# Weight sums of the seven-product stages: from subtracts on VectorE to accumulating DMAs

## The chip, the cores and the metric

The kernel runs on one core of a Trainium2 chip. The metric is the device time of one execution in microseconds (us). A core has TensorE (PE, matmul), VectorE (DVE), ScalarE (ACT), GpSimd (POOL) and SyncE (SP), each with an instruction queue of its own that runs in order, and 16 DMA engines that all queues share.

## The reference

512 tokens of width 1024 run through a first block (three mixers, a gate, the projection `w_o`, a convolved feed-forward network with `w_down`) and through a second block of depth 2 (three branches, the projection `w_out_2`, an MLP of width 4096 with `w_mlp_out_2`). What matters here are the products that end a part and add to the residual:

```python
x = x + merged @ w_o[i]
x = x + conv_ffn(rmsnorm(x, ln2_g[i]), ...)      # (silu(a) * v) @ w_down
```

and their like in the second block. All data are 32-bit floats.

## The kernel before

Every 32-bit operand is split into a high and a low half; a product is then three matmuls (high by high, high by low, low by high). For a weight tile `raw` of 128x1024, `halve` makes both halves by `split`: ACT casts the high half (`whi`, L294), DVE subtracts it from the raw tile and leaves the low half (`wlo`, L295). There are 7 buffers for raw tiles and 5 for each kind of half, given out in turn. Tiles named `pg` hold 128x512 of tokens, features or their halves; `ax`, `mm` and `po` are banks in which PE accumulates.

The method `quick` (from L928) computes a product of 512 tokens by a weight block of `kt` x 128 rows and 1024 columns as seven products of half-size blocks instead of eight. It runs 14 times, and these are the stages of this text: `w_o` once, the feed-forward output three times (ffn 1, 2 and 3, with kt of 8, 8 and 6), `w_out_2` twice (w_out, one for each layer of the second block) and `w_mlp_out_2` eight times (the mlp stages, four for each layer). With b11, b12, b21, b22 for the four quarters of the weight block, two raw tiles each, the right operands are W1 = b11, W2 = b21, W5 = b12 - b11, W6 = W5's tile combined with b22, W3 = b22, W7 = b12's tile combined with b22, W4 = b21 combined with W6's tile. Each quarter is loaded from HBM by SP (`load`, L941), b21 twice, and each combination is a DVE subtract of a 128x1024 tile (`combine`, L949). A combination overwrites a tile in place, after the tile's halves have been made. The left operands (`Forms.make`, from L84) are combined on DVE from the features when these come out of the stage before (L89 to L92) and are split in the same way.

`product` is 24 matmuls (L959 to L961) for each of two banks, one bank for 128 tokens; `add` takes a bank into the residual on DVE (L966, or L968 where a scale is applied). The products run in the order 1, 2, 5, 6, 3, 7, 4, with the last piece of 1 and of 2 after both. Products 6, 7 and 4 go on in the banks of product 1 (`a`), product 3 in those of product 5, so that a bank must have been added before the next product may write on. A scheduler sets the order of the instructions on each engine when the kernel is built. Between product 7 and product 4 the scheduler puts matmuls of the next features (L269 to L271).

Of the kernel before, what the change touches and what calls it, by code (L numbers as in the profile page):

```python
# [13 lines left out]
ALU = mybir.AluOpType  # L14
# [21 lines left out]
class Page:  # L36


    def __init__(self, arena, i, t):
        self.arena, self.i, self.t = arena, i, t  # L40
# [30 lines left out]
class Forms:  # L71

    def __init__(self, body):
        self.body, self.raws, self.blocks, self.pages, self.half = body, [], [], [], None

# [6 lines left out]
    def make(self, r1, r2):  # L85
        B = self.body
        v, c, d = B.nc.vector, slice(0, 256), slice(256, 512)
        s, w = B.pgs(2, True)
        v.tensor_tensor(s.t[:, c], r1.t[:, d], r2.t[:, d], op=ALU.add)  # L89
        v.tensor_tensor(r1.t[:, d], r1.t[:, c], r1.t[:, d], op=ALU.subtract)  # L90
        v.tensor_tensor(s.t[:, d], s.t[:, c], r1.t[:, c], op=ALU.subtract)
        v.tensor_tensor(w.t[:, c], r2.t[:, c], s.t[:, d], op=ALU.subtract)  # L92
        out = []
        for x in (r1, r2, s):
            hi, lo = B.pair(1)
            B.split(hi[0].t, lo[0].t, x.t)
            out.append((hi[0], lo[0]))
            x.free()
        if self.half is None:
            hi, lo = B.pair(1)  # L100
            self.half = (hi[0], lo[0])
            h, o = self.half, c
            self.pages += self.half
        else:
            h, o, self.half = self.half, d, None
        B.split(h[0].t[:, o], h[1].t[:, o], w.t[:, c])
        w.free()
        self.pages += [x for y in out for x in y]
        at = lambda pg, sl: tuple(x.t[:, sl] for x in pg)
        self.blocks.append({1: at(out[0], c), 7: at(out[0], d), 2: at(out[1], c), 4: at(out[1], d), 5: at(out[2], c),  # L110
                            6: at(out[2], d), 3: at(h, o)})
# [6 lines left out]
class Body:  # L118
# [18 lines left out]
    def mm(self):  # L137
        return self.pp.tile([P, 512], F32, tag="mm", name=self.nm("mm"), bufs=3)
# [158 lines left out]
    def turn(self, srcs):  # L297

        pt = self.ax()
        for i, s in enumerate(srcs):  # L300
            self.nc.tensor.transpose(pt[:, i * P:(i + 1) * P], s, self.ident)  # L301
        return pt
# [625 lines left out]
    def quick(self, w, k0, kt, F, X, scale=1.0, rows=None, turn=None):  # L928

        nc, Ls = self.nc, F.blocks
        v = w[k0 * P:(k0 + kt) * P, :].rearrange("(i e p) n -> e p i n", e=2, p=P)
        n = kt // 2
        parts = [(a, min(a + 2, n)) for a in range(0, n, 2)]

        def load(e, h, j):
            a, b = parts[j]
            t = self.raw()[:, :(b - a) * 512]  # L940
            nc.sync.dma_start(t.rearrange("p (k n) -> p k n", n=512), v[e - 1][:, a:b, 512 * (h - 1):512 * h])  # L941
            return t

        def right(ts):
            return [x for t in ts for x in self.halve(t, 512)]

        def combine(out, x, y, op):
            for o, a, b in zip(out, x, y):
                nc.vector.tensor_tensor(o, a, b, op=op)  # L949

        def product(i, W, pss, more=False, a=0, b=n):

            mm = nc.tensor.matmul
            for q, ps in enumerate(pss):
                c = slice(q * P, (q + 1) * P)
                for k in range(a, b):
                    hi, lo = W[k]
                    uh, ul = Ls[k][i]
                    mm(ps, uh[:, c], hi, start=not more and k == 0, stop=False, skip_group_check=more)  # L959
                    mm(ps, uh[:, c], lo, start=False, stop=False, skip_group_check=more)  # L960
                    mm(ps, ul[:, c], hi, start=False, stop=k == n - 1, skip_group_check=more)  # L961

        def add(t, h, y):
            x = X[t][h].t
            if scale == 1.0:
                nc.vector.tensor_tensor(x, x, y, op=ALU.add)  # L966
            else:
                nc.vector.scalar_tensor_tensor(x, y, scale, x, op0=ALU.mult, op1=ALU.add)  # L968

        ss, xn = {}, {}  # L970

        def sums(t):
            if rows:
                ss[t] = self.st(2)
                self.square_sum(X[t][1].t, ss[t][:, 1:2])

        js = range(len(parts))
        two = range(2)
        bank = lambda: [self.ax() for _ in two]
        b11 = [load(1, 1, j) for j in js]  # L980
        W1 = right(b11)
        a = bank()

        product(1, W1, a, b=n - 1)
        W2 = right([load(2, 1, j) for j in js])
        e = [self.mm() for _ in two]
        product(2, W2, e, b=n - 1)
        product(1, W1, a, a=n - 1)
        product(2, W2, e, a=n - 1)
        b12 = [load(1, 2, j) for j in js]  # L990
        combine(b11, b12, b11, ALU.subtract)
        W5 = right(b11)
        d = bank()
        product(5, W5, d)
        for q in two:
            add(q, 0, a[q])
        W6, W3 = [], []
        for j in js:
            t = load(2, 2, j)
            combine([b11[j]], [t], [b11[j]], ALU.subtract)  # L1000
            W6 += right([b11[j]])
            combine([b12[j]], [t], [b12[j]], ALU.subtract)
            W3 += right([t])
        for q in two:
            add(q, 0, e[q])
        product(6, W6, a, more=True)
        for q in two:
            add(2 + q, 1, d[q])
        product(3, W3, d, more=True)
        for q in two:  # L1010
            add(q, 1, a[q])
        W7 = right(b12)
        for q in two:
            add(q, 1, d[q])
            sums(q)
            if rows:
                xn[q] = rows(q, ss[q])
        product(7, W7, a, more=True)
        b21 = [load(2, 1, j) for j in js]
        combine(b21, b21, b11, ALU.subtract)  # L1020
        W4 = right(b21)
        for q in two:
            add(2 + q, 1, a[q])
            sums(2 + q)
            if turn:
                turn(q, xn[q])
        product(4, W4, a, more=True)
        for q in two:
            add(2 + q, 0, a[q])
            if rows:  # L1030
                xn[2 + q] = rows(2 + q, ss[2 + q])
        self.free(F)
        return lambda: [turn(t, xn[t]) for t in (2, 3)] if turn else None
# [727 lines left out]
```

## Time and profile before

| | before |
|---|---|
| median of 3 runs | 2857.28 us (2855.76 to 2858.98) |
| the profiled execution | 2858.8 us, span 2857.0 us |
| PE busy | 2803.2 us (98%) |
| DVE busy | 2012.7 us (70%) |
| ACT busy | 1316.8 us (46%) |
| POOL busy | 386.9 us (14%) |
| the 112 subtracts L949 on DVE | 134.1 us |

The profile is of one execution. Its busy shares are means over the whole span; what a stage waits for is read in the timeline, where a row gives the start, the duration, the engine, the line and the operation, and in square brackets the idle time of the engine ahead of it with what ended that. PE starts the next matmul before the last has left, so that the duration of one matmul (0.39 us) is longer than the distance between two.

### The profile page before, as it was taken

The page shows a single profiled execution, that of the slowest core. Times are in us where ns is not written, and L with a number is a line of the kernel's source. Part 1 is how long each engine was busy: PE and PEld are TensorE (multiplying, and loading weights), DVE is VectorE, ACT ScalarE, POOL GpSimd, SP SyncE. Part 2 cuts the span into 40 slices and gives each one's busy share as a digit, 9 for nine tenths or more (in the row PEclk, how much of TensorE's full clock was granted, in tenths as well). Part 3 has the DMA queues.
Part 4 walks back from the last instruction along what each step waited for, and adds up shares of the span by engine and source line. Part 5 has one row for each costly group of instructions (what it writes and reads, how often), then busy time and mean ns, then how long its engine had stood idle before and what let it go on. Part 6 is the DMA issues. An engine that isn't in the chain of part 4 may idle for free.

```text
span 2857.0 us, 36632 instructions
## 1 busy us (share of the span) xinstructions
PE 2803.2 (98%) x13639; PEld 2344.4 (82%) x13639; DVE 2012.7 (70%) x3585; ACT 1316.8 (46%) x2285; POOL 386.9 (14%) x414
## 2 busy tenths in 40 slices
PE   8999999999999999999999999999999999999999
PEld 7888888888878777888888788888888878788887
DVE  4346466758788786865767887777775767877777
ACT  4344245434444355553455444445554356444444
POOL 0002102400000005210631000002321343000000
PEclk9999999999999999999999999999999999999999
DMA  7243332234232433122222523344232222334432
GB/s 224 84 125 98 105 96 66 81 103 150 87 111 82 136 109 115 60 88 82 75 60 59 155 90 96 117 129 157 72 92 62 75 75 59 106 108 125 132 119 67
DMA packets 225655, 288.19 MB, mean 101 GB/s; under 512 B 17770, under 2 KB 155332, under 8 KB 225476
## 3 DMA queue, kind: packets, MB, share of 16 engines
q1 hardware_dynamic: 212288, 272.77, 31.3%
q10 hardware_dynamic: 13187, 13.08, 1.5%
q8 instruction: 107, 1.75, 0.3%
q14 instruction: 73, 0.59, 0.1%
HBM read 276.30 MB, written 11.67 MB: 101 GB/s over the span
## 4 chain that ended last, share of the span: by engine, by line
PE 85%; DVE 8%; POOL 3%; DMA 2%; issue 1%; ACT 1%; ACTq 0%; SPq 0%; POOLq 0%; DVEq 0%
PE mm L270 16%; PE mm L269 16%; PE mm L271 16%; PE ax L959 4%; PE ax L961 4%; PE ax L960 4%; PE mm L280 4%; PE mm L282 4%; PE mm L281 4%; PE ax L301 3%; DVE wlo L295 2%; POOL stats L312 1%; PE po L1343 1%; PE ax L1247 1%; PE ax L1248 1%
## 5 line engine op out<-in xcount | busy, mean ns | idle before, releaser
L295 DVE TENSOR_TENSOR wlo<-raw,whi 128x1024 fp32r<-128x1024 f32 (+3 forms) x554 | 668.9, 1214 | 314.5 <-ACT whi L294 309.5
L294 ACT CAST whi<-raw 128x1024 fp32r<-128x1024 f32 (+3 forms) x554 | 569.4, 1032 | 652.3 <-PE mm L270 353.6
L269 PE MATMUL mm<-uh,whi 128*128 128x512 f32 (+1 forms) x1792 | 686.4, 384 | 3.9 <-ACT uh L294 3.9
L270 PE MATMUL mm<-ul,whi 128*128 128x512 f32 (+1 forms) x1792 | 684.8, 382 | 3.6 <-DVE stats L311 1.8
L271 PE MATMUL mm<-uh,wlo 128*128 128x512 f32 (+1 forms) x1792 | 683.7, 383 | 0.0
L269 PEld LDWEIGHTS mm<-uh,whi 128*128 128x128 f32 x1792 | 336.9, 188 | 69.9 <-ACT uh L294 5.3
L270 PEld LDWEIGHTS mm<-ul,whi 128*128 128x128 f32 x1792 | 337.8, 189 | 68.3 <-DVE ul L295 2.6
L271 PEld LDWEIGHTS mm<-uh,wlo 128*128 128x128 f32 x1792 | 337.9, 189 | 65.2 <-issue 1.2
L280 PE MATMUL mm<-whi,uh 128*128 128x512 f32 (+3 forms) x736 | 279.8, 382 | 1.1 <-ACT uh L294 0.8
L282 PE MATMUL mm<-whi,ul 128*128 128x512 f32 (+3 forms) x736 | 278.3, 379 | 2.4 <-DVE ul L295 2.4
L281 PE MATMUL mm<-wlo,uh 128*128 128x512 f32 (+3 forms) x736 | 278.5, 379 | 0.4 <-DVE wlo L295 0.4
L959 PE MATMUL ax<-whi,pg 128*128 128x512 f32 x660 | 253.6, 392 | 8.2 <-DVE pg L966 4.2
L960 PE MATMUL ax<-wlo,pg 128*128 128x512 f32 x660 | 255.7, 390 | 0.0
L961 PE MATMUL ax<-whi,pg 128*128 128x512 f32 x660 | 252.9, 392 | 1.0 <-DVE pg L295 1.0
L312 POOL TENSOR_TENSOR stats<-stats,mhalf 128x1 f32<-128x1 f32 (+3 forms) x84 | 91.0, 1087 | 1193.5 <-DVE stats L327 612.8
L294 ACT CAST pg<-pg 128x512 fp32r<-128x512 f32 (+2 forms) x264 | 145.4, 574 | 140.4 <-DVE pg L1660 44.8
L301 PE MATMUL ax<-c_k_ident,pg 128*128 128x128 f32 x993 | 151.6, 279 | 25.4 <-DVE pg L335 10.1
L295 DVE TENSOR_TENSOR pg<-pg,pg 128x512 fp32r<-128x512 f32 (+2 forms) x264 | 160.3, 629 | 6.2 <-ACT pg L294 5.8
L301 PEld LDWEIGHTS ax<-c_k_ident,pg 128*128 128x128 f32 x993 | 123.5, 144 | 49.1 <-POOL pg L1212 11.0
L282 PEld LDWEIGHTS mm<-whi,ul 128*128 128x128 f32 x736 | 139.3, 189 | 25.6 <-DVE ul L295 3.1
L280 PEld LDWEIGHTS mm<-whi,uh 128*128 128x128 f32 x736 | 139.7, 190 | 24.6 <-ACT uh L294 1.2
L281 PEld LDWEIGHTS mm<-wlo,uh 128*128 128x128 f32 x736 | 139.7, 190 | 23.1 <-DVE wlo L295 0.6
(264 smaller groups left out, 4147.6 us busy)
## 6 DMA issues: line engine op xcount, KB each, us to landing
raw<-in_w_in_dram SPq DMA_DIRECT2D x180, 512.0 KB
raw<-in_w_mlp_out_dram SPq DMA_DIRECT2D x80, 512.0 KB
raw<-in_w_mlp_in_dram SPq DMA_DIRECT2D x64, 512.0 KB
raw<-in_ffn_w_up_dram SPq DMA_DIRECT2D x44, 512.0 KB
raw<-in_ffn_w_down_dram SPq DMA_DIRECT2D x25, 512.0 KB
raw<-in_w_out_dram SPq DMA_DIRECT2D x20, 512.0 KB
raw<-in_w_branch_dram SPq DMA_DIRECT2D x16, 512.0 KB
raw<-in_w_o_dram SPq DMA_DIRECT2D x10, 512.0 KB
```

What stands on the lines that cost most here:

```text
L269: mm(ps, hi[:, cols], uh, start=k == 0, stop=False)
L270: mm(ps, hi[:, cols], ul, start=False, stop=False)
L271: mm(ps, lo[:, cols], uh, start=False, stop=k == nk - 1)
L280: mm(ps, uh, hi, start=k == 0, stop=False)
L281: mm(ps, uh, lo, start=False, stop=False)
L282: mm(ps, ul, hi, start=False, stop=k == n - 1)
L294: self.nc.scalar.copy(hi, src)
L295: self.nc.vector.tensor_tensor(lo, src, hi.bitcast(F32), op=ALU.subtract)
L301: self.nc.tensor.transpose(pt[:, i * P:(i + 1) * P], s, self.ident)
L959: mm(ps, uh[:, c], hi, start=not more and k == 0, stop=False, skip_group_check=more)
L960: mm(ps, uh[:, c], lo, start=False, stop=False, skip_group_check=more)
L961: mm(ps, ul[:, c], hi, start=False, stop=k == n - 1, skip_group_check=more)
```

## The change

The right operands are now sums, made by DMAs that add what they fetch to what stands in the tile. x holds b11 at first; after its halves are made (W1), a DMA from GpSimd's queue adds b12 (W5 = b11 + b12), then b22 (W6), then b21 (W4). A second pair of tiles z holds b22 (W3), and b12 is added to it (W7). W2 = b21 has tiles of its own. All 112 DVE subtracts at L949 are gone. A stage with two raw tiles per quarter now has 6 loads on SP and 8 accumulating DMAs on GpSimd (`onto`) where it had 10 loads. So that the sums serve, signs move: two subtracts of `Forms.make` become scalar_tensor_tensor with a factor of -1, another swaps its operands, and `add` subtracts in the right half of the columns. The matmuls are the same in number and shape. Lines behind L73 move by one, those of `product` and `add` by five (L964 to L966, L971 and L973); the accumulating DMA is L942.

```diff
-        v.tensor_tensor(s.t[:, c], r1.t[:, d], r2.t[:, d], op=ALU.add)
+        v.tensor_tensor(s.t[:, c], r2.t[:, d], r1.t[:, d], op=ALU.subtract)
...
-        v.tensor_tensor(s.t[:, d], s.t[:, c], r1.t[:, c], op=ALU.subtract)
-        v.tensor_tensor(w.t[:, c], r2.t[:, c], s.t[:, d], op=ALU.subtract)
+        v.scalar_tensor_tensor(s.t[:, d], s.t[:, c], -1.0, r1.t[:, c], op0=ALU.mult, op1=ALU.subtract)
+        v.scalar_tensor_tensor(w.t[:, c], r2.t[:, c], -1.0, s.t[:, d], op0=ALU.mult, op1=ALU.subtract)
...
+        def move(eng, t, e, h, j, **kw):
+            a, b = parts[j]
+            eng.dma_start(t.rearrange("p (k n) -> p k n", n=512), v[e - 1][:, a:b, 512 * (h - 1):512 * h], **kw)
+            return t
...
+        def onto(ts, e, h):
+            for j, t in enumerate(ts):
+                move(nc.gpsimd, t, e, h, j, accum_op=ALU.add)
...
-        def combine(out, x, y, op):
-            for o, a, b in zip(out, x, y):
-                nc.vector.tensor_tensor(o, a, b, op=op)
...
-                nc.vector.tensor_tensor(x, x, y, op=ALU.add)
+                nc.vector.tensor_tensor(x, x, y, op=ALU.subtract if h else ALU.add)
...
-        b11 = [load(1, 1, j) for j in js]
-        W1 = right(b11)
+        x = [load(1, 1, j) for j in js]
+        W1 = right(x)
+        onto(x, 1, 2)
...
-        b12 = [load(1, 2, j) for j in js]
-        combine(b11, b12, b11, ALU.subtract)
-        W5 = right(b11)
+        W5 = right(x)
+        onto(x, 2, 2)
...
-        for j in js:
-            t = load(2, 2, j)
-            combine([b11[j]], [t], [b11[j]], ALU.subtract)
-            W6 += right([b11[j]])
-            combine([b12[j]], [t], [b12[j]], ALU.subtract)
-            W3 += right([t])
+        z = [load(2, 2, j) for j in js]
+        W6 = right(x)
+        onto(x, 2, 1)
+        W3 = right(z)
+        onto(z, 1, 2)
...
-        W7 = right(b12)
+        W7 = right(z)
...
-        b21 = [load(2, 1, j) for j in js]
-        combine(b21, b21, b11, ALU.subtract)
-        W4 = right(b21)
+        W4 = right(x)
```

The first place is PE in ffn 1, from the last matmuls of product 1 (into `ax716` and `ax717`) to the first of product 6, which writes on in `ax716`. Before:

```order
L960 MATMUL ax733_6820<-wlo731_6816,pg508_6723 128x512
L961 MATMUL ax716_6741<-whi714_6737,pg505_6716 128x512
L961 MATMUL ax717_6742<-whi714_6737,pg505_6716 128x512
L961 MATMUL ax732_6819<-whi730_6815,pg509_6724 128x512
L961 MATMUL ax733_6820<-whi730_6815,pg509_6724 128x512
L959 MATMUL ax716_6741<-whi735_6850,pg456_6209 128x512
```

Now, where the same banks are called `ax712` and `ax713`:

```order
L966 MATMUL ax712_6735<-whi710_6729,pg505_6708 128x512
L966 MATMUL ax713_6736<-whi710_6729,pg505_6708 128x512
L964 MATMUL ax727_6810<-whi722_6799,pg474_6373 128x512
L964 MATMUL ax726_6809<-whi724_6803,pg508_6715 128x512
...
L965 MATMUL ax727_6810<-wlo725_6804,pg508_6715 128x512
L966 MATMUL ax727_6810<-whi724_6803,pg509_6716 128x512
L964 MATMUL ax712_6735<-whi730_6841,pg456_6201 128x512
```

More of product 5 (the banks `ax732` and `ax733` before, `ax726` and `ax727` now) stands between the two: 13 matmuls lie between the last one into the first bank and the first one of product 6, where 3 did.

The second place is DVE in the second mlp stage, around the adds of product 1's banks (`ax1612`, `ax1613`; now `ax1588`, `ax1589`). Before:

```order
L295 TENSOR_TENSOR wlo1634_15263<-raw1630_15254,whi1633_15262 128x1024
L966 TENSOR_TENSOR pg1095_13646<-pg1095_13646,ax1612_15148 128x512
L966 TENSOR_TENSOR pg1097_13648<-pg1097_13648,ax1613_15149 128x512
L949 TENSOR_TENSOR raw1645_15368<-raw1645_15368,raw1607_15138 128x1024
L966 TENSOR_TENSOR pg1095_13646<-pg1095_13646,mm1620_15180 128x512
L295 TENSOR_TENSOR wlo1637_15270<-raw1607_15138,whi1636_15269 128x1024
L966 TENSOR_TENSOR pg1097_13648<-pg1097_13648,mm1621_15181 128x512
L966 TENSOR_TENSOR pg1100_13651<-pg1100_13651,ax1628_15226 128x512
L295 TENSOR_TENSOR wlo1639_15275<-raw1635_15266,whi1638_15274 128x1024
L966 TENSOR_TENSOR pg1102_13653<-pg1102_13653,ax1629_15227 128x512
L295 TENSOR_TENSOR wlo1641_15333<-raw1622_15212,whi1640_15332 128x1024
L295 TENSOR_TENSOR wlo1643_15337<-raw1623_15214,whi1642_15336 128x1024
```

Now (`raw1582` and `raw1583` are x, `raw1604` and `raw1605` z):

```order
L296 TENSOR_TENSOR wlo1607_15209<-raw1582_15088,whi1606_15208 128x1024
L971 TENSOR_TENSOR pg1095_13614<-pg1095_13614,ax1588_15102 128x512
L296 TENSOR_TENSOR wlo1609_15213<-raw1583_15090,whi1608_15212 128x1024
L971 TENSOR_TENSOR pg1097_13616<-pg1097_13616,ax1589_15103 128x512
L971 TENSOR_TENSOR pg1095_13614<-pg1095_13614,mm1596_15134 128x512
L296 TENSOR_TENSOR wlo1611_15219<-raw1604_15204,whi1610_15218 128x1024
L971 TENSOR_TENSOR pg1100_13619<-pg1100_13619,ax1602_15176 128x512
L971 TENSOR_TENSOR pg1097_13616<-pg1097_13616,mm1597_15135 128x512
L296 TENSOR_TENSOR wlo1613_15223<-raw1605_15206,whi1612_15222 128x1024
...
L296 TENSOR_TENSOR wlo1615_15283<-raw1604_15204,whi1614_15282 128x1024
...
L296 TENSOR_TENSOR wlo1617_15287<-raw1605_15206,whi1616_15286 128x1024
```

W6's two low halves stand at the first two adds, then W3's two, then W7's; W3's first low half has about the place that the L949 had.

The third place is POOL's queue in the first layer of the second block, between the powers of the norm (`mhalf`) ahead of the four mlp stages and what follows. Before, nothing of those stages stands there:

```order
L1575 TENSOR_SCALAR pg1036_13017<-pg1036_13017,stats_116 128x512
L312 TENSOR_TENSOR stats_116<-stats_116,mhalf_144 128x1 x8
L312 TENSOR_TENSOR stats_116<-stats_116,mhalf_144 128x8
L1196 TENSOR_TENSOR pg1348_16833<-pg1348_16833,hg1809_16776 128x512
L1211 TENSOR_TENSOR pg1348_16833<-pg1350_16842 128x8x8
```

Now:

```order
L313 TENSOR_TENSOR stats_116<-stats_116,mhalf_144 128x1 x4
L942 DMA raw1510_14460<-in_w_mlp_out_2_dram 128x2x512
L942 DMA raw1511_14462<-in_w_mlp_out_2_dram 128x2x512
L942 DMA raw1510_14460<-in_w_mlp_out_2_dram 128x2x512
L942 DMA raw1511_14462<-in_w_mlp_out_2_dram 128x2x512
L942 DMA raw1510_14460<-in_w_mlp_out_2_dram 128x2x512
L942 DMA raw1511_14462<-in_w_mlp_out_2_dram 128x2x512
L942 DMA raw1532_14576<-in_w_mlp_out_2_dram 128x2x512
L942 DMA raw1533_14578<-in_w_mlp_out_2_dram 128x2x512
L942 DMA raw1582_15088<-in_w_mlp_out_2_dram 128x2x512
```

Eight accumulating DMAs of a stage stand one behind the other, six onto x and then two onto z, and the next stage's follow at once.

## Rows read from the trace of the kernel before

**Rows 1.** The page's busy time, share of the span and instructions of each engine

```profile
PE 2803.2 (98%) x13639; PEld 2344.4 (82%) x13639; DVE 2012.7 (70%) x3585; ACT 1316.8 (46%) x2285; POOL 386.9 (14%) x414
```

**Rows 2.** Groups by line: busy us, mean ns | idle us before, its releasers

```profile
L949 DVE TENSOR_TENSOR raw<-raw,raw 128x1024 f32<-128x1024 f32 (+1 forms) x112 | 134.1, 1199 | 6.1 <-DMA raw<-in_w_out_dram 1.9 <-DMA raw<-in_w_o_dram 1.8 <-DMA raw<-in_ffn_w_down_dram 1.0
...
L966 DVE TENSOR_TENSOR pg<-pg,ax 128x512 f32<-128x512 f32 x132 | 87.9, 680 | 35.1 <-PE ax L961 34.9
...
L968 DVE SCALAR_TENSOR_TENSOR pg<-ax,pg 128x512 f32<-128x512 f32 x36 | 23.9, 682 | 1.1 <-PE ax L961 1.1
```

**Rows 3.** PE's timeline in ffn 1, ffn 3 and w_out: where it waits

```profile
819.50 0.73 PE L961 MATMUL ax<-whi,pg 128*128 128x512 f32 x2 [0.36 <-DVE pg L295]
821.57 0.50 PE L959 MATMUL ax<-whi,pg 128*128 128x512 f32 x1 [1.33 <-DVE pg L966]
...
1047.53 0.73 PE L961 MATMUL mm<-whi,pg 128*128 128x512 f32 x2 [0.57 <-DVE pg L295]
1049.65 0.50 PE L959 MATMUL ax<-whi,pg 128*128 128x512 f32 x1 [1.39 <-ACT pg L294]
...
1066.99 0.47 PE L959 MATMUL ax<-whi,pg 128*128 128x512 f32 x1 [1.29 <-DVE pg L966]
...
1608.84 0.50 PE L959 MATMUL ax<-whi,pg 128*128 128x512 f32 x1 [1.34 <-DVE pg L968]
```

**Rows 4.** Windows around ffn 1 and an mlp stage: us, busy us of each engine

```profile
800.00:847.10 47.10, 45.41 (x200) 36.96 (x199) 37.64 (x47) 19.02 (x22) 0.00 (x0) 1.00 0.48 145
1765.62:1807.27 41.65, 41.65 (x185) 34.51 (x184) 31.93 (x40) 17.23 (x19) 0.00 (x0) 1.00 0.49 152
```

(The columns are PE, PEld, DVE, ACT, POOL, then granted clock, DMA share and GB/s.)

**Rows 5.** DVE's timeline in ffn 1, ahead of the waits of PE

```profile
815.55 1.23 DVE L295 TENSOR_TENSOR wlo<-raw,whi 128x1024 fp32r<-128x1024 f32 x1 [0.43 <-ACT whi L294]
...
817.63 1.22 DVE L949 TENSOR_TENSOR raw<-raw,raw 128x1024 f32<-128x1024 f32 x1
818.76 0.68 DVE L295 TENSOR_TENSOR pg<-pg,pg 128x512 fp32r<-128x512 f32 x1
...
820.84 1.87 DVE L966 TENSOR_TENSOR pg<-pg,ax 128x512 f32<-128x512 f32 x3
```

**Rows 6.** Timeline of an mlp stage: DVE, ACT and PE

```profile
1777.63 1.22 DVE L295 TENSOR_TENSOR wlo<-raw,whi 128x1024 fp32r<-128x1024 f32 x1
...
1784.92 1.22 DVE L295 TENSOR_TENSOR wlo<-raw,whi 128x1024 fp32r<-128x1024 f32 x1
...
1785.09 1.06 ACT L294 CAST whi<-raw 128x1024 fp32r<-128x1024 f32 x1 [1.84 <-PE ax L961]
...
1794.41 0.39 PE L960 MATMUL ax<-wlo,pg 128*128 128x512 f32 x1
```

**Rows 7.** Loads: SP's issues of L941, a load in the chain of waits, DMA queue

```profile
L941 SPq DMA_DIRECT2D raw<-in_w_mlp_out_dram x80: 367/368/368, 1628.2 to 2826.3; - x80
...
1584.88 3.48 DMA raw<-in_w_out_dram
...
GB/s 14 209 223 85 361 0 0 0 0 0 0 0 7 274 166 153 300 0 82 347 17 148 305 190 251 174 268 178 255 78 333 133 341 44 126 318 170 264 14 0
...
q1 hardware_dynamic: 212288, 272.77, 31.3%
```

(The first gives minimum, median and maximum ns; the third what the DMAs moved in 40 slices of 800 to 847 us; the last packets, MB and the share of 16 engines over the span.)

**Rows 8.** POOL by line, and POOL beside DVE in the timeline

```profile
L1211 POOL TENSOR_TENSOR pg<-pg 128x64 f32<-128x64 f32 (+3 forms) x64 | 51.7, 808 | 146.2 <-DVE pg L1210 76.5 <-issue 29.2 <-DVE stats L1264 16.4
...
1122.47 1.30 POOL L1196 TENSOR_TENSOR pg<-pg,hg 128x512 f32<-128x512 f32 x1 [0.90 <-DVE pg L1195]
...
1133.64 2.11 POOL L1196 TENSOR_TENSOR pg<-pg,hg 128x512 f32<-128x512 f32 x1 [0.90 <-DVE pg L1195]
...
1128.49 2.48 DVE L295 TENSOR_TENSOR wlo<-raw,whi 128x1024 fp32r<-128x1024 f32 x2
1133.39 3.44 DVE L295 TENSOR_TENSOR wlo<-raw,whi 128x1024 fp32r<-128x1024 f32 x2
```

**Rows 9.** DVE's and PE's timeline in w_out of the first layer

```profile
1611.03 1.21 DVE L295 TENSOR_TENSOR wlo<-raw,whi 128x1024 fp32r<-128x1024 f32 x1
...
1621.68 0.39 PE L960 MATMUL ax<-wlo,pg 128*128 128x512 f32 x1
```

More of the change, by code (lines that the diff above doesn't have):

```diff
@@ L936, in quick @@
         parts = [(a, min(a + 2, n)) for a in range(0, n, 2)]
+        def move(eng, t, e, h, j, **kw):
+            a, b = parts[j]
+            eng.dma_start(t.rearrange("p (k n) -> p k n", n=512), v[e - 1][:, a:b, 512 * (h - 1):512 * h], **kw)
+            return t
         def load(e, h, j):
             a, b = parts[j]
-            t = self.raw()[:, :(b - a) * 512]
-            nc.sync.dma_start(t.rearrange("p (k n) -> p k n", n=512), v[e - 1][:, a:b, 512 * (h - 1):512 * h])
-            return t
+            return move(nc.sync, self.raw()[:, :(b - a) * 512], e, h, j)
+        def onto(ts, e, h):
+            for j, t in enumerate(ts):
+                move(nc.gpsimd, t, e, h, j, accum_op=ALU.add)
         def right(ts):
             return [x for t in ts for x in self.halve(t, 512)]
-        def combine(out, x, y, op):
-            for o, a, b in zip(out, x, y):
-                nc.vector.tensor_tensor(o, a, b, op=op)
         def product(i, W, pss, more=False, a=0, b=n):
@@ L965, in add @@
             if scale == 1.0:
-                nc.vector.tensor_tensor(x, x, y, op=ALU.add)
+                nc.vector.tensor_tensor(x, x, y, op=ALU.subtract if h else ALU.add)
             else:
-                nc.vector.scalar_tensor_tensor(x, y, scale, x, op0=ALU.mult, op1=ALU.add)
+                nc.vector.scalar_tensor_tensor(x, y, -scale if h else scale, x, op0=ALU.mult, op1=ALU.add)
         ss, xn = {}, {}
@@ L996, in quick @@
             add(q, 0, a[q])
-        W6, W3 = [], []
-        for j in js:
-            t = load(2, 2, j)
-            combine([b11[j]], [t], [b11[j]], ALU.subtract)
-            W6 += right([b11[j]])
-            combine([b12[j]], [t], [b12[j]], ALU.subtract)
-            W3 += right([t])
+        z = [load(2, 2, j) for j in js]
[3 more added lines that the diff above has]
+        onto(z, 1, 2)
         for q in two:
```

## The prediction, made before the changed kernel ran

> **What bounds the kernel now.** I read the page's busy table first: TensorE (PE) is busy 98% of the span, VectorE (DVE) 70%, ScalarE (ACT) 46%, GpSimd (POOL) 14% [rows 1]. Next the groups by line: the combining subtracts of L949 cost DVE 134.1 us in 112 pieces [rows 2]. They count only where PE waits for DVE. So I went through PE's timeline of all 14 seven-product stages, looking for idle time. It stands in five of them [rows 3]: ffn 1 has 0.36 + 1.33 = 1.69 us, ffn 2 the same, ffn 3 0.57 + 1.39 + 1.29 and a small one of 0.20, 3.45, w_out 1.34 in the first layer, 1.34 and a small one of 0.25 in the second; together 9.76 us. The w_o stage and the eight w_mlp_out stages have none: in the stretch of one of the latter PE is busy 41.65 of 41.65 us, DVE 31.93, while the stretch around ffn 1 has PE 45.41 of 47.10 [rows 4]. The chance of gain is thus small: 9.8 us of 2857, and the 134 us of DVE are a cover, not a path.
>
> **The sum's frame.** Durations come from the profiled execution: 2858.8 us for a span of 2857.0, 1.5 above the median 2857.28. I work out a difference against 2858.8 and carry it to the median.
>
> **Removed: 112 subtracts (L949), 56 loads on SP.** In ffn 1 the 1.33 us wait is for the add L966, which starts at 820.84 behind a queue on DVE; the L949 of 817.63 stands in that queue after DVE's last idle moment (0.43 us at 815.55) and takes 817.63 to 818.76, 1.13 us [rows 5]. Without it the add starts 1.13 earlier. Besides, the order changes: between product 1's last matmul into its first bank and product 6's first into the same bank stand 3 matmuls before and 13 now. At the pitch of PE (185 matmuls in 41.65 us [rows 4], 0.225 us each) ten more give 2.3 us. 1.13 + 2.3 = 3.4 us of cover against 1.69: both waits of ffn 1 go, and by the same pattern ffn 2's. The two w_out stages wait in the same place for L968, and I count them whole too: 1.69 + 1.69 + 1.34 + 1.59 = 6.3 us. In ffn 3 the 1.39 us is put down to ACT's cast of a left block, not to a subtract, and 1.29 to an add late in the stage; I take half, 1.7 of 3.45. Sum: 8.0 us; ends 4.7 (one of the four waits stays, ffn 3 gives nothing) and 9.8. What is late next in those stages is nothing that I see: PE's next operands are covered by a full product (24 matmuls, 5.4 us). In the nine other stages the subtracts hid beside PE, and taking them away gives nothing. The 56 loads cost SP's queue 0.368 us each to issue [rows 7], beside other work: nothing.
>
> **Signs.** Two of the left blocks' subtracts become scalar_tensor_tensor, and some adds subtract. The one form costs 682 ns where the other costs 680 [rows 2]: nothing.
>
> **Added: 112 accumulating DMAs on POOL's queue.** The trace of before has no such DMA, so I bound it. What is queued behind a waiting accumulate on POOL: in the mlp stages only the next accumulate, since in before nothing stands there between the norm's powers at the two ends of a layer; in the last stage of a block the norm's L312, which come after product 3's adds, when all accumulates of the stage have been issued. The issue on POOL: SP's 0.37 below, 1.3 (a 128x512 operation of POOL) above; I take 0.8, the mean of L1211 [rows 7, 8]. The latency: a load in the chain of waits took 3.48 us [rows 7]. The rate: the fastest slice moved 361 GB/s, so a tile of 0.524 MB keeps the 16 engines 1.45 us; the mean of the main queue, 31.3% of 2857 us for 272.77 MB, makes that 1.72 [rows 7]. An accumulate reads two operands, so it takes between 1.45 (the second read beside the first) and 2 x 1.72 = 3.44. I take 2.2, the middle between 1.45 and 2.90. What is left of 3.48 after issue (0.37) and transfer (1.45) is a fixed 1.66.
>
> **The room for it.** I looked at each chain of halves in DVE's and ACT's timeline; the tightest is z += b12 in the mlp stages. z's second tile can be added to once its low half is made (L295 that starts 1784.92, ends 1786.14 [rows 6]; in the changed order the low half of W3 takes the subtract's place, so I keep this time). It must be there for the cast of W7's second tile: product 7 needs its low half by the matmul of 1794.41, so the cast must start by 1794.41 - 1.22 - 1.06 = 1792.1. Room 6.0 us. In w_out of the first layer, read the same way, it is 1611.03 + 1.21 = 1612.2 to 1621.68 - 1.22 - 1.06 = 1619.4 [rows 9], 7.2; there W3's low half comes 1.13 earlier without the L949 ahead of it and PE 1.34 earlier without its wait: 7.0. The ffn stages I take to be no tighter. But four accumulates share the queue in this time. Their tiles come free at about 1778.85 (x, first; DVE's L295 of 1777.63), 1781.4, 1783.8 and 1786.1 (pitches 1.13 for L295, 0.60 for L966, in the new order). With 0.8 + 1.66 ahead and 2.2 each, the first ends at 1783.5, the second 1786.1, the third 1788.5, the last 1790.8, which is 1.3 ahead of 1792.1: **exposed 0**. With 3.44 each (fixed part 1.39 then) they queue: 1781.04 + 4 x 3.44 = 1794.8, **2.7 late**. With 2.90 they end at 1792.9, 0.8 late. It begins to cost at about 2.7 us each. Below nothing it cannot go: PE has no idle time in these stages to give back. Cost, if late: eight mlp stages, where nothing else hides it.
>
> **A row that speaks against POOL.** In POOL's timeline an L1196 alone takes 1.30 us; one that ran beside two low halves of DVE took 2.11, and those took 3.44 instead of 2.48 [rows 8]. So each slows the other, and DVE runs such halves through all of these stages. I keep this as a rival below. The Trainium skill (SBUF — State Buffer, section "SBUF: two separate sides") warns of a trap for DMAs issued from GpSimd: while VectorE holds the port pair that the two share, GpSimd cannot write the descriptors, the DMA engines idle, and it advises to issue from another queue. By that rule each accumulate would wait for the end of a DVE operation, and the sum would be the rival's; by the forecast it is 2850. Nothing in this trace shows whether an accumulate's issue is such a case.
>
> **The rivals.**
> *A, the forecast.* The waits go, the accumulates are covered: 2858.8 - 8.0 = 2850.8, carried to the median 2849.3; I say 2850. Ends: 2857.3 - 9.8 - 1.5 (the spread of the runs) = 2846, 2857.3 - 4.7 = 2852.6.
> *B, something else is late in their place.* The low half of W6's first tile now stands in front of the first bank's add on DVE, and waits for its own accumulate; so product 6's bank may come free as late as before. Against it: the accumulates of W5 to W6 are the only ones in flight then. Then half to all of the gain stays away: 2853 to 2857.
> *C, the accumulates run at half the rate* (two reads, one after the other); the case that ends on the other side. For it: an accumulate has twice the reads. Against it: the mean DMA share of a stage is 0.49 [rows 4], so the engines have time. Place: the cast of W7's second tile. 2.7 us late in eight stages, 21.6, and 2.7 - 1.0 = 1.7 in the six others with a room of about 7, of which I count three, 5: 2857.3 - 8 + 27 = 2876. The gain is used up when the eight are 8/8 = 1 us late, just above 2.9 us for each accumulate; at 2.9 it is 2857.3 - 8 + 6.4 = 2856, the same as before.
> *D, POOL waits for DVE.* If each issue waits out one low half (1.22) and itself takes 0.81 longer (2.11 - 1.30), it costs 2.8 instead of 0.8, one behind the other: the fourth is out at 1778.85 + 4 x 2.8 = 1790.05, done at 1790.05 + 1.66 + 2.2 = 1793.9, 1.8 late, 14 in eight stages: 2857.3 - 8 + 14 = 2864. Waiting out a pair (2.48), 4.1 each, it would be 7 late, which I leave outside. If only the 0.81 comes on top, the last is done at 1791.6 and covered.
> That the change doesn't do what it says can be excluded: no combining subtract is left in DVE's order.
>
> **How the numbers follow.** A 0.43, B 0.14 (same), C 0.22 (0.14 slower, 0.08 same), D 0.21 (0.15 slower, 0.06 same). What a measurement of this kernel tells from no change is about 0.2%, 5.7 us: 2851.6 to 2863.0. Faster 0.43, same 0.28, slower 0.29. The likeliest case gives **2850**, its own range 2846 to 2853. The range takes in B, C and most of D: 2846 to 2880; left out are D at its full price and what I don't see, 0.15.
>
> **What would show it.** In the changed trace: the waits at the places of [rows 3] gone in ffn 1, ffn 2 and w_out (steps of the removal); DVE busy down by 134 us to about 1879, and POOL's queue showing 112 issues (the size of 0.8); in an mlp stage PE busy for the whole of it, as in [rows 4]; an accumulate's time from the end of L295 to the cast below 6 us (rate and room). Wrong it would be if PE sits idle in product 7 for ACT's cast of W7, which waits for a DMA: with tiles 3.4 us apart this is C, with POOL's issues starting late or long beside DVE's low halves it is D. Waits that stay at the adds L971 and L973 in the ffn stages are B.

## The result: 1% slower, and the profile after

The changed kernel takes 2885.0 us (median of 4 runs, 2883.5 to 2893.1) where before takes 2857.1: a ratio of 1.0103, 95% interval 1.0083 to 1.0123. The forecast was 2850, with a range up to 2880. The profiled execution of after is the longest of its four runs (2893.1 us, span 2891.3; its mean granted clock is 0.989, theirs 0.992 to 0.993), so that its trace shows some 8 us more than the median.

The page's busy times and DMA queues of after answer to [rows 1] and to the last of [rows 7]:

```profile
PE 2820.0 (98%) x13639; PEld 2353.8 (81%) x13639; DVE 1895.6 (66%) x3473; ACT 1309.3 (45%) x2285; POOL 523.1 (18%) x526
...
q1 hardware_dynamic: 197312, 243.93, 27.6%
q0 software_dynamic: 29952, 57.68, 12.4%
```

DVE's busy time has fallen by 117 us, not by the 134 that the prediction gave as a sign (to about 1879). Part of the difference is overlap. The 134.1 counts each subtract from its start to its end, and on a full queue the next operation starts before that end: in [rows 5] the subtract of 817.63 lasts 1.22 us, and 818.76 follows 1.13 after its start. PE's 13639 matmuls are the same, but it is busy 16.8 us longer (2820.0 against 2803.2) and idle 17.5 us longer (span less busy: 71.3 against 53.8). Where, the start of product 1 in each stage tells (first matmul of the stage in PE's timeline):

| stage | before | after | difference | change over what lies before |
|---|---|---|---|---|
| w_o | 669.45 | 668.79 | -0.7 | |
| ffn 1 | 803.11 | 808.93 | +5.8 | w_o: +6.5 |
| ffn 2 | 930.51 | 934.05 | +3.5 | ffn 1: -2.3 |
| ffn 3 | 1037.73 | 1037.41 | -0.3 | ffn 2: -3.9 |
| w_out, layer 1 | 1587.96 | 1590.04 | +2.1 | ffn 3 and the branches: +2.4 |
| mlp 1 | 1684.03 | 1696.96 | +12.9 | **w_out: +10.9** |
| mlp 4 | 1928.83 | 1942.72 | +13.9 | mlp 1 to 3: +1.0 |
| w_out, layer 2 | 2475.40 | 2495.18 | +19.8 | mlp 4 and the branches: +5.9 |
| mlp 1 | 2570.31 | 2601.71 | +31.4 | **w_out: +11.6** |
| mlp 4 | 2815.11 | 2847.40 | +32.3 | mlp 1 to 3: +0.9 |
| end of span | 2857.0 | 2891.3 | +34.3 | mlp 4: +2.0 |

ffn 1 and 2 gained 6.2 us, more than the 3.4 of the forecast. The six mlp stages within a layer, the place of the rival that I feared, cost 1.9 us together. The loss is in the six stages that end a part, w_o, ffn 3, the two w_out and the two last mlp stages, and two thirds of it in w_out.

PE's timeline of after in w_out of the first layer, then of the last mlp stage of that layer (columns as in [rows 3]):

```profile
1612.52 0.77 PE L964 MATMUL ax<-whi,pg 128*128 128x512 f32 x1 [3.27 <-ACT whi L295]
1633.57 1.32 PE L302 MATMUL ax<-c_k_ident,pg 128*128 128x128 f32 x8 [1.69 <-DVE pg L336]
1636.12 0.76 PE L964 MATMUL ax<-whi,pg 128*128 128x512 f32 x1 [1.23 <-DVE pg L973]
...
1971.52 0.50 PE L964 MATMUL ax<-whi,pg 128*128 128x512 f32 x1 [1.41 <-ACT whi L295]
1972.78 0.50 PE L965 MATMUL ax<-wlo,pg 128*128 128x512 f32 x1 [0.76 <-DVE wlo L296]
```

The wait of 1.34 us in [rows 3] is not gone: it has grown to 3.27. Both stand ahead of the first matmul of product 6, behind 72 of the stage's 168 matmuls (a product is 24, 12 for each of its two banks). Two waits are new, at the end of the stage, where the transposes of the norm (L302) and product 4 stand. In the last mlp stage PE waits in product 7, for W7's halves: the sign that the prediction gave for being wrong.

What product 6 waits for is in DVE's and ACT's timeline of after just before 1612.52:

```profile
1606.57 1.23 DVE L296 TENSOR_TENSOR wlo<-raw,whi 128x1024 fp32r<-128x1024 f32 x1 [4.49 <-ACT whi L295]
1610.55 1.23 DVE L296 TENSOR_TENSOR wlo<-raw,whi 128x1024 fp32r<-128x1024 f32 x1 [2.75 <-ACT whi L295]
1611.69 1.88 DVE L973 SCALAR_TENSOR_TENSOR pg<-ax,pg 128x512 f32<-128x512 f32 x3
...
1605.49 1.05 ACT L295 CAST whi<-raw 128x1024 fp32r<-128x1024 f32 x1 [4.26 <-DMA raw<-in_w_out_dram]
1609.47 2.94 ACT L295 CAST whi<-raw 128x1024 fp32r<-128x1024 f32 x3 [2.93 <-DMA raw<-in_w_out_dram]
```

ACT waits for W6's two accumulates, DVE waits for ACT, and the adds of product 1's banks (L973) wait behind W6's low halves on DVE, although PE's last matmul had ended 2.4 us before (1612.52 - 3.27 = 1609.25). Product 6 cannot start until its bank is added, by the first of these three adds, which ends at 1612.37. The bracket at 1612.52 names ACT, because the last of the three casts of 1609.47 happens to end just after, at 1612.41; that cast is W3's. How long an accumulate takes is in the view of line L942: POOL's time for the issue (minimum, median, maximum ns), and the time from issue to landing in three stretches of after, all 112 first, then W6's two of this w_out, then six in an mlp stage (1780 to 1799 us):

```profile
L942 POOL DMA_DIRECT2D raw<-in_w_mlp_out_dram x64: 1203/1203/1214, 1679.4 to 2867.2; - x64
...
DMA to landing us min/median/max: 3.9/6.0/10.6
...
DMA to landing us min/median/max: 8.4/9.5/10.6
...
DMA to landing us min/median/max: 5.7/5.8/6.4
```

In the mlp stage an accumulate lands 5.8 us after its issue begins, although up to three others are in flight beside it; the one that product 6 waited for took 10.6.

About half of the loss is PE's clock: the same matmuls keep PE busy 16.8 us longer. Windows of after behind the waits at 707.57, 1070.12, 1612.52, 1636.12 and 2540.99 (us, PE busy and its matmuls, granted clock, DMA share, GB/s):

```profile
707.57:709.90 2.33, 2.33 (x6) 0.50 0.94 312
1070.12:1075.40 5.28, 5.28 (x13) 0.50 0.74 223
1612.52:1617.80 5.28, 5.28 (x13) 0.50 0.90 135
1636.12:1641.90 5.78, 5.78 (x14) 0.50 0.60 185
2540.99:2546.30 5.31, 5.31 (x13) 0.50 0.61 171
```

A clock of 0.50 is 1.2 instead of 2.4 GHz. 13 matmuls took 5.28 us; at the pitch of [rows 4], 0.225, they take 2.9. The four longer stretches cost 2.4 to 2.6 us each, the first 1.0 in its window, beside the waits ahead of them (1.23 to 4.32). Not all of it comes with the change: behind the norm's waits in the branches, which the change does not touch, the clock was low for longer too (granted clock 0.56 from 1427.5 to 1435.0 of after, 0.76 from 1427.0 to 1434.0 of before). The length of the wait alone does not decide it: behind a wait of 3.26 us in the second w_out (2517.64 us) the clock stayed at 1.00.

### The profile page after: what moved, and what is told of

Its sections match the earlier page's. It is cut to its first block, busy times and chain, and to the rows that moved or that the text cites. A ratio compares the mean times of both kernels' runs of the same rounds, so it can differ in the third digit from the quotient of the medians.

```text
span 2891.3 us, 36818 instructions
## 1 busy us (share of the span) xinstructions
PE 2820.0 (98%) x13639; PEld 2353.8 (81%) x13639; DVE 1895.6 (66%) x3473; ACT 1309.3 (45%) x2285; POOL 523.1 (18%) x526
## 3 DMA queue, kind: packets, MB, share of 16 engines
q1 hardware_dynamic: 197312, 243.93, 27.6%
q0 software_dynamic: 29952, 57.68, 12.4%
## 4 chain that ended last, share of the span: by engine, by line
PE 69%; issue 14%; DMA 7%; DVE 6%; POOL 2%; ACT 1%; ACTq 0%; POOLq 0%; SPq 0%; DVEq 0%
PE mm L271 12%; PE mm L272 12%; PE mm L270 12%; PE mm L281 4%; PE mm L283 4%; PE mm L282 4%; DMA raw<-in_w_mlp_out_dram 4%; PE ax L302 3%; PE ax L964 2%; PE ax L965 2%; PE ax L966 2%; DVE wlo L296 2%; DMA raw<-in_w_out_dram 1%; PE po L1344 1%; PE ax L1248 1%
## 5 line engine op out<-in xcount | busy, mean ns | idle before, releaser
L964 PE MATMUL ax<-whi,pg 128*128 128x512 f32 x660 | 261.3, 401 | 22.8 <-ACT whi L295 10.2
L965 PE MATMUL ax<-wlo,pg 128*128 128x512 f32 x660 | 262.4, 399 | 3.8 <-DVE wlo L296 3.8
L966 PE MATMUL ax<-whi,pg 128*128 128x512 f32 x660 | 257.0, 397 | 0.0
L302 PE MATMUL ax<-c_k_ident,pg 128*128 128x128 f32 x993 | 152.4, 280 | 28.7 <-DVE pg L336 15.5
L942 POOL DMA_DIRECT2D raw<-in_w_mlp_out_dram x64 | 77.0, 1204 | 551.5 <-DVE wlo L296 544.0
L964 PEld LDWEIGHTS ax<-whi,pg 128*128 128x128 f32 x660 | 127.1, 193 | 55.2 <-ACT whi L295 13.6
L302 PEld LDWEIGHTS ax<-c_k_ident,pg 128*128 128x128 f32 x993 | 123.5, 145 | 53.5 <-DVE pg L336 17.7
```

## The experiments

The theories: the accumulates of W6 and W7 come late in the stages that end a part, because other transfers share the DMA engines there (contention); or because even an undisturbed accumulate is too slow for these stages; or the accumulates are not the cause, and the signs or the new order are.

**Sums on DVE, signs as changed.** The stages as before, with `add` for `subtract`:

```diff
+        def plus(out, y):
+            for o, b in zip(out, y):
+                nc.vector.tensor_tensor(o, o, b, op=ALU.add)
...
-        onto(x, 1, 2)
...
+            b12 = [load(1, 2, j) for j in js]
+            plus(x, b12)
```

and likewise for W6, W7 and W4. W4 is made in W6's tile, as in the changed kernel.

> All 14 stages make the same sums with the new signs, but by an extra load on SP and an add on DVE instead of an accumulating DMA. Theory (the accumulates are the cost: they land in 5.9 us alone and in 7 to 10.6 us beside other transfers in the stages that end a part): 2855 to 2860, like before. Rival (the signs cost, by scalar_tensor_tensor and subtracting adds, or by the order that they bring): 2870 or more.

Measured 2850.4 us, ratio 0.9977 (0.9968 to 0.9987). Without accumulates the whole loss is gone, so it is not the signs. Unexpected: this kernel, which does before's work with other signs and with W4 in W6's tile, is 5.6 us faster than before. DVE's timeline shows why, in ffn 1, where [rows 5] had the subtract of 817.63 ahead of the add:

```profile
817.84 2.47 DVE L975 TENSOR_TENSOR pg<-pg,ax 128x512 f32<-128x512 f32 x4
820.23 1.22 DVE L958 TENSOR_TENSOR raw<-raw,raw 128x1024 f32<-128x1024 f32 x1
```

(L975 is the add, L958 the sum.) The adds come first. PE's waits of 0.36 and 1.33 us shrink to one of 0.31.

**The order by itself.** The kernel before with one edit: W4's subtract writes onto W6's tile.

```diff
-        combine(b21, b21, b11, ALU.subtract)
-        W4 = right(b21)
+        combine(b11, b21, b11, ALU.subtract)
+        W4 = right(b11)
```

> The kernel before, with its own signs and subtracts, but W4's subtract writes onto W6's tile instead of b21's. The operations are the same in number and kind; the scheduler's order on DVE differs from before in 253 places and from that of the kernel with DVE sums and new signs in 2. Theory (the 5.6 us by which DVE sums with new signs beat before come from the order on DVE, in ffn 1 and 2 above all): 2849 to 2852. Rival (they come from the signs): 2856.

Measured 2851.0 us, ratio 0.9983 (0.9974 to 0.9992). PE's wait in ffn 1 is then 0.28 us, and DVE's timeline there has the same order as above, with a subtract in place of the sum:

```profile
817.86 2.47 DVE L966 TENSOR_TENSOR pg<-pg,ax 128x512 f32<-128x512 f32 x4
820.25 1.22 DVE L949 TENSOR_TENSOR raw<-raw,raw 128x1024 f32<-128x1024 f32 x1
```

So the gain in ffn 1 and 2 does not need the subtracts gone: most of it comes with the order that the scheduler finds when W4 is made in W6's tile, with all 112 subtracts still there.

**No accumulates in the stages that end a part.** The same DVE sums there only (a stage has `rows` when a norm or the output follows it).

```diff
+        if rows is None:
+            x = [load(1, 1, j) for j in js]
+            W1 = right(x)
+            onto(x, 1, 2)
...
+        else:
...
```

> Accumulating DMAs only in the eight stages that end no part (ffn 1 and 2, the first three mlp stages of each layer); sums on DVE in the other six. Theory: ffn 1 and 2 keep the 6.3 us that they gained, the mlp stages pay 1 to 2: 2851 to 2853. Rival (the accumulates disturb what comes after them too, by their use of the DMA engines): 2857 or more.

Measured 2848.0, ratio 0.9968 (0.9956 to 0.9981), 3 us below the range that I gave. With no accumulates at all it was 2850.4: those of the eight other stages do no harm.

**The residual's reload earlier.** In the second block the 8 pages of 256 KB that w_out adds to are reloaded just ahead of it. In after SP issues six of them from 1591.18 on and two from 1597.37, beside W6's accumulates. Here they go earlier; SP issues them from 1499.5 to 1549.0.

```diff
-        mg = self.alone(gc)
         H = [self.pgs(2) for _ in range(NT)]
         for t in range(NT):
             for h in range(2):
                 nc.sync.dma_start(H[t][h].t, self.hd[...])
+        mg = self.alone(gc)
```

> The changed kernel, with the reload of the residual ahead of w_out (8 transfers of 256 KB) put earlier in the program, ahead of the last gate of the branches. Theory (contention on the DMA engines lengthens W6's accumulates in w_out from 6 to 10.6 us): W6's accumulates in w_out land in 6 to 7 us, the two waits of 3.3 us ahead of product 6 go, with the slow clock behind each (2.7 us): 2885 - 12 = 2873. Rival (even 6 us is too long there, since the adds stand behind W6's low halves on DVE): the waits stay above 2 us, 2881 to 2885.

Measured 2877.0, ratio 1.0070 (1.0056 to 1.0083): 8 us of the 12. The landing of W6's two accumulates of w_out, and PE's waits in that stage:

```profile
DMA to landing us min/median/max: 5.8/6.1/6.4
...
1622.66 0.50 PE L965 MATMUL ax<-wlo,pg 128*128 128x512 f32 x1 [0.27 <-DVE wlo L296]
1630.63 1.32 PE L302 MATMUL ax<-c_k_ident,pg 128*128 128x128 f32 x8 [2.69 <-DVE pg L336]
1633.18 0.77 PE L964 MATMUL ax<-whi,pg 128*128 128x512 f32 x1 [1.23 <-DVE pg L973]
```

The wait of 3.27 ahead of product 6 is gone, in both layers. The reload was the cause of that one: 10.6 us became 6.4. The end of the stage stays late, and DVE's timeline of this kernel shows what it hangs on:

```profile
1615.16 2.07 DVE L973 SCALAR_TENSOR_TENSOR pg<-ax,pg 128x512 f32<-128x512 f32 x3
1621.38 1.23 DVE L296 TENSOR_TENSOR wlo<-raw,whi 128x1024 fp32r<-128x1024 f32 x1 [4.15 <-ACT whi L295]
1622.52 0.68 DVE L973 SCALAR_TENSOR_TENSOR pg<-ax,pg 128x512 f32<-128x512 f32 x1
```

DVE stands still for 4.15 us for W7's first low half. Behind it in DVE's queue are the stage's remaining adds (1622.52) and the first step of the norm (L328, at 1626.27), and the transposes and product 4 wait for these. In a stage within a part no norm follows, and PE goes on with the next features. In the second mlp stage of after DVE stands still for W7 as long, and the stage takes no longer than before (81.60 us from its product 1 to that of the next):

```profile
1803.36 1.23 DVE L296 TENSOR_TENSOR wlo<-raw,whi 128x1024 fp32r<-128x1024 f32 x1 [4.17 <-ACT whi L295]
```

In the first w_out of the kernel with the early reload W7's accumulates still take 7.3 and 7.6 us; in the second they land in 5.9 and 6.2, and PE still waits there at the transposes and at product 4:

```profile
DMA to landing us min/median/max: 5.9/6.1/6.2
...
2526.84 1.32 PE L302 MATMUL ax<-c_k_ident,pg 128*128 128x128 f32 x8 [1.86 <-DVE pg L336]
2529.39 0.47 PE L964 MATMUL ax<-whi,pg 128*128 128x512 f32 x1 [1.23 <-DVE pg L973]
```

So contention made W6 late in w_out, and at the end of the second w_out even accumulates that landed in some 6 us were too late for W7. Which of the two it is in w_o, ffn 3 and the last mlp stages no run tests by itself.

**W7 alone, W6 alone, W6 and W7 on DVE, in the six stages that end a part.** Three kernels. W7: `z` gets b12 by a load and a DVE add. W6: `x` gets b22 by a DVE add of `z`. The third does both, so that only W5 and W4 are accumulated there.

```diff
         W3 = right(z)
-        onto(z, 1, 2)
+        if rows is None:
+            onto(z, 1, 2)
+        else:
+            for o, b in zip(z, [load(1, 2, j) for j in js]):
+                nc.vector.tensor_tensor(o, o, b, op=ALU.add)
```

> The changed kernel, with W7 alone summed on DVE (b12 loaded once more) in the six stages that end a part; W5, W6 and W4 by accumulating DMAs. Theory: the wait of 3.3 us ahead of product 6 in w_out stays with its slow clock, the waits at the end of w_o, ffn 3, w_out and the MLP, which come from DVE's queue standing still for W7's low halves, shrink: 2885 - 18 = 2867. Rival (the late end comes from W6 alone, which delays all that follows): 2880 or more.

> The changed kernel, with W6 alone summed on DVE (from the loaded b22) in the six stages that end a part; W5, W7 and W4 by accumulating DMAs. Theory (two separate late places): the wait of 3.3 us ahead of product 6 goes, the waits at the end of the stages stay: 2885 - 14 = 2871. Rival (W6 alone): about 2850, like the kernel with W5 and W4 only.

> In the six stages that end a part only W5 and W4 are made by accumulating DMAs (room 13 us and more); W6 and W7 are summed on DVE from loaded tiles. The other eight stages are as in the changed kernel. Theory (W6 and W7 are what is late): the six stages lose their new waits, and with half the DVE sums of before also a part of the old ones: 2847 to 2853. Rival (any accumulate in these stages costs, W5 and W4 too): 2858 or more.

| on DVE at the ends | median us | ratio to before |
|---|---|---|
| none (after) | 2885.0 | 1.0103 (1.0083 to 1.0123) |
| W7 | 2861.7 | 1.0019 (1.0009 to 1.0030) |
| W6 | 2862.5 | 1.0020 (1.0011 to 1.0029) |
| W6 and W7 | 2848.0 | 0.9967 (0.9955 to 0.9980) |

Each alone gives more than I expected (23 against 18, 23 against 14), and both together 37, not the sum of 46. PE's timeline of the first w_out shows two separate places: with W7 on DVE (first two rows) the wait ahead of product 6 stays and the end comes nearly in time, with W6 on DVE (last three) it is the other way round.

```profile
1604.76 0.47 PE L964 MATMUL ax<-whi,pg 128*128 128x512 f32 x1 [2.47 <-ACT whi L295]
1622.22 0.47 PE L964 MATMUL ax<-whi,pg 128*128 128x512 f32 x1 [0.86 <-DVE stats L328]
```

```profile
1600.64 0.50 PE L964 MATMUL ax<-whi,pg 128*128 128x512 f32 x1 [0.29 <-DVE pg L973]
1619.88 0.47 PE L964 MATMUL ax<-whi,pg 128*128 128x512 f32 x1 [2.62 <-DVE pg L973]
1624.17 0.50 PE L964 MATMUL ax<-whi,pg 128*128 128x512 f32 x1 [0.41 <-DVE pg L973]
```

That the singles overlap would fit a chain, in which a late W6 pushes W7's start and so the end; this is not shown. In the traces of the kernels with one of the two the clock stayed at 1.00 behind the waits of w_out, which would be part of the 23 us. How large a part is open: these traces are of executions of 2857.2 and 2859.2 us, 3 to 5 under their medians, and that of after is 8 over its own.

**Without W4's accumulates.** b21 is then missing in W4.

```diff
         W6 = right(x)
-        onto(x, 2, 1)
         W3 = right(z)
```

> The changed kernel without the two accumulating DMAs of W4 in every stage (b21 is not added, so product 4 works on W6's blocks again). In the changed kernel they stand ahead of W7's in POOL's queue. Theory A (accumulates share the DMA engines, so that W4's delay W7's): W7's accumulates in w_out land in 5.9 to 6.3 us instead of 7.6 and 8.4, the stage that ends the MLP from 8.1 to 6, and the waits at the end of those stages shrink: 2885 - 8 = 2877. Theory B (W7's accumulates are late for other reasons): 7 us and more as before, 2882 to 2886.

Measured 2882.5, ratio 1.0088 (1.0074 to 1.0101): 2.5 us less than after, with overlapping intervals. W7's two accumulates in the first w_out land in 5.9 and 6.7 us instead of 7.6 and 8.4, so accumulates do delay one another; but in the second layer's w_out one still takes 8.1, and the time hardly moves. So W4's accumulates are not the cause.

**Two attempts at the best.** First the kernel with W6 and W7 on DVE at the ends, but with all sums of ffn 3 on DVE (`if kt == 8:` ahead of the one form, `else:` the other). Then W6 and W7 on DVE in all 14 stages, in effect:

```diff
-        onto(x, 2, 2)
...
-        W6 = right(x)
-        onto(x, 2, 1)
-        W3 = right(z)
-        onto(z, 1, 2)
+        plus(x, z)
+        W6 = right(x)
+        onto(x, 2, 1)
+        W3 = right(z)
+        plus(z, [load(1, 2, j) for j in js])
```

> Like the kernel with W5 and W4 by accumulating DMA in the stages that end a part, but ffn 3 with all its sums on DVE, since it kept a wait of 3.4 us there. If that wait and its slow clock are from ffn 3's accumulates: 2848 - 3 = 2845. If not: 2848.

> W5 and W4 by accumulating DMAs in all 14 stages, W6 and W7 summed on DVE in all of them. Theory (an accumulate costs nothing where its room is over 10 us, and the ones of W6 and W7 gain nothing in the mlp stages): 2847 to 2850, as with W6 and W7 by accumulates in the eight other stages. Rival (the gain of ffn 1 and 2 comes from W6's and W7's accumulates): 2851 to 2854.

Measured 2848.2, ratio 0.9968 (0.9956 to 0.9979), and 2849.9, ratio 0.9975 (0.9965 to 0.9984). The first did not bring the 3 us: the wait of 3.38 us ahead of product 4 of ffn 3 is 1.22 there, but the norm behind it waits 6.04, where the other kernel's three waits behind that place came to 4.06: 7.3 against 7.4 in all. The second is as its theory had it. The best three kernels (2848.0, 2848.0 and 2848.2) cannot be told apart; all beat both kernels, by 8 to 9 us against before and 37 against after. Of the 9, the order alone has about 5 (2855.7 - 2851.0 = 4.7, the two measured side by side).

## Why the prediction was wrong, point by point

- **What bounds the kernel** held: 9.8 us of waits were to be had, and no kernel's median was under 2847.9.
- **The removal** held in ffn 1 and 2, where no wait is left (6.2 us in the table, 3.4 of it the waits themselves, 1.7 the clock behind one of them). The reason was only half right: the subtract was in the way by its place in DVE's queue, and another order of the same work frees PE too.
- **W_out and ffn 3**, 4.6 us of the forecast gain: wrong. The wait ahead of product 6 in w_out went from 1.34 to 3.27 us, the one ahead of product 4 in ffn 3 from 1.29 to 4.32.
- **The cost of an accumulate** was mis-sized. POOL's issue is 1.20 us, not 0.8 (the upper end was 1.3); to landing it is 5.8 in an mlp stage, where my terms 0.8 + 1.66 + 2.2 make 4.7. These 1.1 us alone lie within the 1.3 that the forecast had to spare in the mlp stages. Its share of the DMA engines is near the upper bound: 12.4% of 2891 us for 57.68 MB is 6.2 us per MB, against 3.3 for the plain queue (27.6%, 243.93 MB), 1.9 times as much.
- **The room in the mlp stages**, 6.0 us, was on the safe side. In the second of them z's second low half ends at 1798.00 and the cast of W7 starts at 1804.80, 6.8 us later, where the prediction's sign was less than 6, and PE did not wait. Six of these stages cost 1.9 us together with accumulates of 5.5 to 6.9 us. So rival C had the share of the engines nearly right and its effect wrong: at 3.44 us per tile I had put each of these stages 2.7 us late.
- **The step that failed** is the sentence in which I gave w_out a room of 7.0 for W7, took the ffn stages "to be no tighter", and set W5 to W6 aside. In the first w_out W7's accumulates took 7.6 and 8.4 us, more than that room, and W6's 8.4 and 10.6. I never worked out W6 in w_out, nor asked what else is in flight there: SP reloads 2 MB of the residual in these microseconds, and with that moved away W6's took 5.8 and 6.4. I also measured each room to PE's next use alone. At the end of a part DVE's queue holds more behind a waiting low half: the last adds and the norm, for which PE waits next. The latency of 5.8 us was priced where it is best hidden, in the stages that repeat, and carried to the six that don't.
- **Rival B** is what happened, in w_out, at a price that I had not seen: adds of finished banks stood behind W6's low halves on DVE. I had it as a return to before, with a loss of gain at most; it had no bound, since an accumulate beside other transfers took 10.6 us.
- **Rival D** fell: the issues on POOL take 1203, 1203 and 1214 ns (minimum, median, maximum) in the mlp stages. One of them, between 1785.24 and 1786.44 us of after, ran wholly beside low halves on DVE, whose two inputs are both in SBUF, and took the same 1.20:

```profile
1784.86 1.62 DVE L296 TENSOR_TENSOR pg<-pg,pg 128x512 fp32r<-128x512 f32 x3
...
1785.24 1.20 POOL L942 DMA_DIRECT2D raw<-in_w_mlp_out_dram  x1 [2.73 <-DVE wlo L296]
```

The Trainium skill (SBUF — State Buffer, section "SBUF: two separate sides") limits the lock for DVE operations with two SBUF inputs to GpSimd operations that read SBUF; writing descriptors showed no such delay here, and I had drawn the rule too wide.

- **Not in the sum at all**: the half clock behind a wait, up to 2.6 us at each of several places. Before had such a stretch already, behind the wait of 1.33 us in ffn 2 (at 948.96, a place that [rows 3] leaves out):

```profile
949.30:952.30 3.00, 3.00 (x9) 0.51 0.51 172
```

Until the pitch is back at 0.23, at 952.95, the matmuls there lose 1.7 us. Ffn 1 has no such stretch ([rows 4]: clock 1.00), and ffn 2 gained 1.6 us more, 3.9 against 2.3.

## What to carry to other kernels

An operation that is cheap on an engine with time to spare should not be replaced by a transfer unless the latency fits in every stage; the stage that ends a part is the one to cost first, since there the in-order queue holds the last adds and the norm behind the wait, and the next part's loads share the DMA engines. A transfer with a room of over 10 us can be accumulated at no cost that these runs show: with W5 and W4 alone in the six stages (2848.0 us) the casts in w_o, the first w_out and the last mlp stage of its layer start 10.6 to 18.3 us after the issues. One with 6 to 7 us cost little where PE had the next features to go on with (1.9 us in six mlp stages), and it was late at the end of a part. And before a gain is put down to the work that was removed, the same work in another order should be tried: here that alone gave half of it.

## What the runs showed of the hardware

An accumulating DMA of 512 KB from HBM onto an SBUF tile, issued from POOL, took 1.20 us of POOL and 5.8 us to land in an mlp stage (5.5 to 6.9 in six of them), 8.4 and 10.6 us beside the reload of the residual in w_out, and held the DMA engines 1.9 times as long per byte as a plain load. Of 256 KB (ffn 3's second tile) the issue took 0.90 us and the landing 3.9 us at the least. Waits of PE of 1.2 to 4.3 us were followed by 2 to 6 us at 1.2 GHz in five places of after, and one of 3.26 us (2517.64) by none.
